# A two-layer hybrid encoder on one core: hi|lo side by side in the feed-forward, and the recurrence's cross-block products taken together

## Chip, core and metric

The kernel runs on one core of a Trainium2 chip. The metric is the device time of one execution in microseconds (us), median over the runs. In the profile TensorE is PE (its weight loads are PEld), VectorE is DVE, ScalarE is ACT, GpSimd is POOL, and SyncE, whose queue issues the weight DMAs, is SP. PSUM is the memory that TensorE writes its products to, in banks of 512 fp32 columns; the other operands lie in SBUF.

## What is computed

Two layers work on a residual stream x of 256 tokens by 1024 channels. Each layer projects x, runs three token mixers (pooling, windowed attention, and a gated linear recurrence in both directions), gates and merges them, and normalises. Then comes the feed-forward, 2816 wide:

```python
hidden = jax.nn.silu(x1 @ w_ffn_gate[i]) * (x1 @ w_ffn_up[i])
ffn = hidden @ w_ffn_down[i]
```

The recurrence, for 8 heads of 128 channels, with decays f = exp(log_f):

```python
b = jnp.cumsum(log_f)                 # within a chunk
att = (q * exp(b)) @ (k * exp(-b)).T  # kept where s <= t
o_intra = tril(att) @ v
o_inter = (q * exp(b)) @ state        # then: state = decay * state + kd.T @ v
```

It runs once forward and once over the flipped sequence, and both results are added. All operands are fp32.

## The kernel before

**Split operands.** A projection takes each fp32 operand as a hi and a lo part, both of type float32r, and computes hi x hi + hi x lo + lo x hi, three matmuls into one PSUM bank (`mm3`, lines 250 to 254). The activation's parts are the tiles `xh` and `xl`, [128, 8, 256] each: 8 blocks of 128 channels by 256 tokens.

**Weights.** All weights are listed as 214 chunks of 1 MB in the order of their use (lines 139 to 181). A chunk goes through three steps: `dma_chunk` issues its DMA on SP's queue into `raw`; `split_chunk` makes `whi` by a ScalarE copy (line 210) and `wlo` by a VectorE subtraction (line 211), and issues the DMA three chunks on; a product uses it (`use_chunk`). raw, whi and wlo have three buffers each, so the split of a chunk writes the buffer of the chunk that has just been used.

**Two forms of product.** `gemm_cols` (line 256) has weights stationary and 256 tokens moving: for two column blocks m and 8 channel blocks k, three matmuls of 256 columns into one half of a bank. `gemm_tok` (line 272) has activations stationary and 512 weight columns moving.

**The feed-forward** (lines 869 to 879): eleven pairs of products a layer, gate and up, each a `gemm_cols` into one bank of the pool `g`. ScalarE applies SiLU to the gate bank (line 873), VectorE multiplies it by the up bank (line 876), and `split_to` makes the hi part (ScalarE, line 293) and the lo part (VectorE, line 294) for the down projection.

**Background work.** Mixers are Python generators in the list `tasks`. After a projection `step_end` splits the next chunk and calls `background` (line 225): it draws on the first three tasks in turn until the costs that they yield reach a budget of 3000; `yield None` puts a task to sleep until the next step. This sets the order in which instructions are written; a list scheduler then orders each engine's instructions by readiness and by that priority.

**The recurrence** (`hgrn_task`, line 348) is one task for each two heads, four in a layer. The list `busy` lets one task at a time into its first part. For each direction d, VectorE forms decay products by two scans (Ct, Rt), two reciprocals into a tile `inv`, and from them QI, KI (inside a block of 64 tokens) and QL, KL (across blocks), tiles of a pool of seven buffers (`work`). After a sleep TensorE computes, all in plain fp32 (two matmul instructions a product): eight diagonal products of 64x64 (line 431), which alternate between the lower and the upper half of the output's partitions; four products of neighbouring blocks (line 439), the forward direction's all on the lower half, the backward direction's all on the upper one; and two products of 128x128 for blocks further apart (line 444). Then the task sleeps, and the other direction follows. At the end masks are applied, two products with v follow (lines 468, 469), a root mean square is formed with POOL's power (line 302, called at 478), the gate product is made (line 484), and the result is turned by TensorE (line 492).

## Time and profile before

| | |
|---|---|
| median of 3 runs | 1334.33 us (1334.32 to 1334.39) |
| the profiled execution | 1334.35 us |
| its span, first to last instruction | 1332.6 us |
| TensorE matmul, busy share | 98% |
| VectorE | 65% |
| ScalarE | 44% |
| POOL | 1% |
| mean granted TensorE clock | 0.996 of full speed |
| moved by DMA | 233 MB, 175 GB/s |

A share is that of the span. Matmuls are pipelined and their ends are modelled, so the distance between the starts of two is what they cost, and not the duration shown. The chain that ended last is followed back from the last instruction: at each step to whatever released it.

### The profile page before, as it was taken

What the parts mean: (1) busy time and instruction counts of PE and PEld (TensorE: products, weight loads), DVE (VectorE), ACT (ScalarE), POOL (GpSimd) and SP (SyncE); (2) the same over time, 40 slices, a digit from 0 to 9 for tenths busy, and PEclk for the clock granted to TensorE, in tenths of its full rate; (3) what the DMA queues carried; (4) which work ended last, traced back from release to release, by engine and by line L of the source; (5) the groups of instructions that cost most, each with busy time, mean ns of one, the idle gap of its engine ahead of it and who ended that gap; (6) DMA issues with size and microseconds to landing.
All of it is one profiled execution on the core that took longest, in us unless ns stands there. A gap on an engine that the chain in (4) does not pass through costs nothing.

```text
span 1332.6 us, 20047 instructions
## 1 busy us (share of the span) xinstructions
PE 1308.5 (98%) x8585; PEld 1185.8 (89%) x8585; DVE 867.5 (65%) x1126; ACT 587.1 (44%) x644; POOL 16.7 (1%) x24
## 2 busy tenths in 40 slices
PE   8999999999999999999989999999999999999997
PEld 6899999998888799998779999999988887999986
DVE  4598887575656855554555999875846658554445
ACT  5444444544444443443334444445534444444431
POOL 0000000000000000000000000000000000000000
PEclk9999999999999999999989999999999999999999
DMA  8654545244556475655356555442455664755551
GB/s 310 196 185 158 166 151 159 96 158 159 197 190 228 151 233 179 189 190 190 126 176 203 169 172 166 158 159 90 134 189 190 202 217 154 226 189 190 180 194 38
DMA packets 160280, 233.43 MB, mean 175 GB/s; under 512 B 3840, under 2 KB 108864, under 8 KB 160192
## 3 DMA queue, kind: packets, MB, share of 16 engines
q1 hardware_dynamic: 158496, 227.44, 51.6%
q10 hardware_dynamic: 1696, 4.72, 1.1%
q8 instruction: 67, 1.10, 0.3%
q14 instruction: 21, 0.17, 0.0%
HBM read 231.10 MB, written 1.05 MB: 174 GB/s over the span
## 4 chain that ended last, share of the span: by engine, by line
PE 93%; DVE 4%; ACT 1%; issue 1%; POOL 1%; DMA 0%; POOLq 0%; DVEq 0%; ACTq 0%
PE g L252 28%; PE g L253 28%; PE g L254 28%; DVE wlo L211 2%; PE t L444 1%; PE t L431 1%; PE t L439 1%; PE t L312 1%; POOL rs_y L302 1%; PE t L468 1%; PE t L469 1%; ACT whi L210 0%; DVE ln_st L326 0%; PE t L508 0%; PE t L528 0%
## 5 line engine op out<-in xcount | busy, mean ns | idle before, releaser
L211 DVE TENSOR_TENSOR wlo<-raw,whi 128x2048 fp32r<-128x2048 f32 (+2 forms) x218 | 489.8, 2249 | 347.4 <-ACT whi L210 347.0
L210 ACT ACTIVATE whi<-raw 128x2048 fp32r<-128x2048 f32 (+2 forms) x218 | 409.9, 1883 | 517.5 <-issue 220.7
L252 PE MATMUL g<-xh,whi 128*128 128x256 f32 x1600 | 455.6, 285 | 0.0
L254 PE MATMUL g<-xh,wlo 128*128 128x256 f32 x1600 | 453.1, 283 | 0.0
L253 PE MATMUL g<-xl,whi 128*128 128x256 f32 x1600 | 453.0, 283 | 0.0
L252 PEld LDWEIGHTS g<-xh,whi 128*128 128x128 f32 x1600 | 307.0, 192 | 0.2
L253 PEld LDWEIGHTS g<-xl,whi 128*128 128x128 f32 x1600 | 307.0, 192 | 0.2
L254 PEld LDWEIGHTS g<-xh,wlo 128*128 128x128 f32 x1600 | 306.9, 192 | 0.0
L252 PE MATMUL g<-whi,xh 128*128 128x512 f32 x480 | 190.2, 397 | 1.3 <-ACT whi L210 1.2
L253 PE MATMUL g<-wlo,xh 128*128 128x512 f32 x480 | 189.5, 395 | 1.4 <-DVE wlo L211 1.4
L254 PE MATMUL g<-whi,xl 128*128 128x512 f32 x480 | 188.1, 393 | 0.0
L253 PEld LDWEIGHTS g<-wlo,xh 128*128 128x128 f32 x480 | 91.8, 191 | 21.4 <-DVE wlo L211 3.1
L252 PEld LDWEIGHTS g<-whi,xh 128*128 128x128 f32 x480 | 91.8, 191 | 21.2 <-ACT whi L210 1.8
L254 PEld LDWEIGHTS g<-whi,xl 128*128 128x128 f32 x480 | 91.6, 191 | 19.1
L253 PE MATMUL g<-wlo,s 128*128 128x512 f32 x224 | 87.5, 391 | 0.0
L254 PE MATMUL g<-whi,s 128*128 128x512 f32 x224 | 87.5, 390 | 0.0
L252 PE MATMUL g<-whi,s 128*128 128x512 f32 x224 | 87.1, 390 | 0.0
L252 PE MATMUL g<-whi,sa 128*128 128x512 f32 x160 | 62.8, 393 | 0.0
L253 PE MATMUL g<-wlo,sa 128*128 128x512 f32 x160 | 62.5, 390 | 0.0
L254 PE MATMUL g<-whi,sb 128*128 128x512 f32 x160 | 62.3, 389 | 0.0
L253 PEld LDWEIGHTS g<-wlo,s 128*128 128x128 f32 x224 | 42.1, 188 | 9.0 <-DVE wlo L211 0.4
L254 PEld LDWEIGHTS g<-whi,s 128*128 128x128 f32 x224 | 42.0, 188 | 8.6
(168 smaller groups left out, 1136.2 us busy)
## 6 DMA issues: line engine op xcount, KB each, us to landing
raw<-in_w_in_dram SPq DMA_DIRECT2D x106, 1024.0 KB, 5.1
raw<-in_w_ffn_gate_dram SPq DMA_DIRECT2D x22, 1024.0 KB, 5.3
raw<-in_w_ffn_up_dram SPq DMA_DIRECT2D x22, 1024.0 KB, 5.3
raw<-in_w_ffn_down_dram SPq DMA_DIRECT2D x22, 1024.0 KB, 4.9
raw<-in_w_branch_c_dram SPq DMA_DIRECT2D x8, 1024.0 KB, 5.1
raw<-in_w_branch_a_dram SPq DMA_DIRECT2D x8, 1024.0 KB, 5.0
raw<-in_w_out_dram SPq DMA_DIRECT2D x8, 1024.0 KB, 4.9
raw<-in_w_ple_gate_dram SPq DMA_DIRECT2D x8, 1024.0 KB, 5.1
```

Source lines behind the costliest of these rows:

```text
L210: A.activation(out=hi[:, ks, :], in_=t[:, ks, :], func=AF.Copy)
L211: V.tensor_tensor(out=lo[:, ks, :], in0=t[:, ks, :], in1=f(hi[:, ks, :]), op=ALU.subtract)
L252: PE.matmul(ps, lhsT=ah, rhs=bh, start=first, stop=False)
L253: PE.matmul(ps, lhsT=ah, rhs=bl, start=False, stop=False)
L254: PE.matmul(ps, lhsT=al, rhs=bh, start=False, stop=last)
L302: G.tensor_tensor(out=y, in0=v, in1=mhalf.to_broadcast([P, n]) if n > 1 else mhalf, op=ALU.pow)
L312: PE.transpose(ps[:, k * P:(k + 1) * P], xt[:, t, (4 * hf + k) * P:(4 * hf + k + 1) * P], ident)
L431: PE.matmul(dg[po:po + 64, co:co + 64], lhsT=KI[:, cs], rhs=QI[:, cs], start=True, stop=True)
L439: PE.matmul(cr[po:po + 64, co:co + 64], lhsT=KL[:, h, 4 * t, :], rhs=QL[:, h, 4 * t, :], start=True, stop=True)
L444: PE.matmul(lg[:, co:co + P], lhsT=kp.rearrange("p b u -> p (b u)"), rhs=qp.rearrange("p b u -> p (b u)"), start=True, stop=True)
L468: PE.matmul(o, lhsT=at[:, 2 * h + t, :], rhs=vt[:, t, hs], start=True, stop=False)
L469: PE.matmul(o, lhsT=al[:, 2 * h + 1 - t, :], rhs=vt[:, 1 - t, hs], start=False, stop=True)
```

## The change

In the feed-forward the gate and up products use a new `gemm_wide`. `xh` and `xl` become two halves of one tile `xx`, [128, 8, 2, 256], so that for each k hi and lo of the activation stand side by side as 512 columns. The hi weights are multiplied by all 512 in one matmul, the lo weights by the 256 hi columns. Each m has a bank of its own; its first half holds hi x hi + lo x hi, its second hi x lo, and `joined` adds them: a ScalarE copy of the first half, then a VectorE addition of the second. The gate's banks come from the pool `g`, the up's from the pool `t`.

In the recurrence the first direction now computes only its diagonal products, and goes on to the second direction without the sleep. The second direction computes the neighbouring-block products of both directions, alternating between the lower and upper half of the output, and then all far ones. `inv` goes: the reciprocals are written into QI and KI and multiplied in place. `tot` becomes a small copy, and KL is allocated after QL has been formed. One sleep is added ahead of the gate product.

```diff
--- before.py
+++ after.py
@@ -260,6 +260,24 @@
                 mm3(ps[:, m * S:(m + 1) * S], (w[0][:, k, ms], w[1][:, k, ms]),
                     act(k), k == 0, k == nk - 1)
 
+    def gemm_wide(w, ps):
+
+
+        for m in range(2):
+            ms = slice(m * P, (m + 1) * P)
+            for k in range(KD):
+                wide = (ps[m], w[0][:, k, ms], xx[:, k].rearrange("p a t -> p (a t)"))
+                narrow = (ps[m][:, 0:S], w[1][:, k, ms], xx[:, k, 0, :])
+                for i, (o, a, b) in enumerate((wide, narrow) if k == 0 else (narrow, wide)):
+                    PE.matmul(o, lhsT=a, rhs=b, start=k == 0 and i == 0, stop=k == KD - 1 and i == 1,
+                              skip_group_check=True)
+
+    def joined(ps, dst):
+
+        for m in range(2):
+            A.activation(out=dst[:, m, :], in_=ps[m][:, 0:S], func=AF.Copy)
+            V.tensor_tensor(out=dst[:, m, :], in0=dst[:, m, :], in1=ps[m][:, S:2 * S], op=ALU.add)
+
     def xk(k):
         return xh[:, k, :], xl[:, k, :]
 
@@ -350,7 +368,7 @@
         while busy:
             yield None
         busy.append(hp)
-        dg = None
+        dg, across = None, []
         smask = kc[:, K_MASK:K_MASK + 512]
         emask = kc[:, K_MASK + 1:K_MASK + 513]
 
@@ -365,7 +383,7 @@
             e, la = (0, 1) if fwd else (1, 0)
             ft, kt = (ff, kf) if fwd else (fb, kb)
             f0 = ft[:, 1:513]
-            Ct, Rt, inv = work([P, 512]), work([P, 512]), work([P, 512])
+            Ct, Rt = work([P, 512]), work([P, 512])
             if fwd:
                 V.tensor_tensor_scan(out=Ct, data0=smask, data1=f0, initial=0.0, op0=ALU.max, op1=ALU.mult)
                 yield 600
@@ -378,29 +396,31 @@
                 V.tensor_tensor_scan(out=Rt, data0=ft[:, 0:512], data1=smask, initial=0.0,
                                      op0=ALU.mult, op1=ALU.max)
             yield 600
-            C, R, I, q3, k3 = c32(Ct), c32(Rt), c32(inv), c32(q), c32(kt)
-            V.reciprocal(out=I[:, :, e, :], in_=R[:, :, e, :])
+            QI, KI = work([P, 512]), work([P, 512])
+            C, R, q3, k3, q2, k2 = c32(Ct), c32(Rt), c32(q), c32(kt), c32(QI), c32(KI)
+            V.reciprocal(out=q2[:, :, e, :], in_=R[:, :, e, :])
             yield 1670
-            V.reciprocal(out=I[:, :, la, :], in_=C[:, :, la, :])
+            V.reciprocal(out=k2[:, :, la, :], in_=C[:, :, la, :])
             yield 1670
-            QI, KI = work([P, 512]), work([P, 512])
-            q2, k2 = c32(QI), c32(KI)
-            V.tensor_tensor(out=q2[:, :, e, :], in0=q3[:, :, e, :], in1=I[:, :, e, :], op=ALU.mult)
+            V.tensor_tensor(out=q2[:, :, e, :], in0=q3[:, :, e, :], in1=q2[:, :, e, :], op=ALU.mult)
             V.tensor_tensor(out=q2[:, :, la, :], in0=q3[:, :, la, :], in1=C[:, :, la, :], op=ALU.mult)
             yield 660
             V.tensor_tensor(out=k2[:, :, e, :], in0=k3[:, :, e, :], in1=R[:, :, e, :], op=ALU.mult)
-            V.tensor_tensor(out=k2[:, :, la, :], in0=k3[:, :, la, :], in1=I[:, :, la, :], op=ALU.mult)
+            V.tensor_tensor(out=k2[:, :, la, :], in0=k3[:, :, la, :], in1=k2[:, :, la, :], op=ALU.mult)
             yield 660
 
             u = 31 if fwd else 0
-            tot = c4(Ct)[:, :, :, :, u:u + 1]
+            tot = small([P, 2, 4, 2, 1], "tot")
+            V.tensor_copy(out=tot, in_=c4(Ct)[:, :, :, :, u:u + 1])
             QL = work([P, 2, 5, 64])
-            KL = work([P, 2, 5, 64])
+            KL = None
             qb = range(1, 4) if fwd else range(0, 3)
             kb_ = range(0, 3) if fwd else range(1, 4)
 
             for L, blks, src, intra, own, far, fac in (
                     (QL, qb, q, QI, e, la, Ct), (KL, kb_, kt, KI, la, e, Rt)):
+                if L is None:
+                    L = KL = work([P, 2, 5, 64])
                 for h in range(2):
                     b0 = blks[0]
                     cs = slice(h * S + 64 * b0, h * S + 64 * b0 + 192)
@@ -429,20 +449,24 @@
                     cs = slice(h * S + 64 * b, h * S + 64 * b + 64)
                     po, co = 64 * (b % 2), d * S + (2 * h + b // 2) * 64
                     PE.matmul(dg[po:po + 64, co:co + 64], lhsT=KI[:, cs], rhs=QI[:, cs], start=True, stop=True)
+            across.append((QL, KL))
             if d == 0:
-                cr, lg = tbank(), tbank()
+                continue
+            cr, lg = tbank(), tbank()
             for h in range(2):
                 for t in range(2):
 
-                    po = 0 if fwd else 64
                     co = (2 * h + t) * 64
-                    PE.matmul(cr[po:po + 64, co:co + 64], lhsT=KL[:, h, 4 * t, :], rhs=QL[:, h, 4 * t, :],
-                              start=True, stop=True)
-                qp = QL[:, h, 2:4, :] if fwd else QL[:, h, 1:3, :]
-                kp = KL[:, h, 1:3, :] if fwd else KL[:, h, 2:4, :]
-                co = (2 * h + d) * P
-                PE.matmul(lg[:, co:co + P], lhsT=kp.rearrange("p b u -> p (b u)"),
-                          rhs=qp.rearrange("p b u -> p (b u)"), start=True, stop=True)
+                    for po, (Q, K) in zip((0, 64), across):
+                        PE.matmul(cr[po:po + 64, co:co + 64], lhsT=K[:, h, 4 * t, :], rhs=Q[:, h, 4 * t, :],
+                                  start=True, stop=True)
+            for h in range(2):
+                for e, (Q, K) in enumerate(across):
+                    qp = Q[:, h, 2:4, :] if e == 0 else Q[:, h, 1:3, :]
+                    kp = K[:, h, 1:3, :] if e == 0 else K[:, h, 2:4, :]
+                    co = (2 * h + e) * P
+                    PE.matmul(lg[:, co:co + P], lhsT=kp.rearrange("p b u -> p (b u)"),
+                              rhs=qp.rearrange("p b u -> p (b u)"), start=True, stop=True)
             if d == 1:
                 busy.clear()
             yield None
@@ -477,6 +501,7 @@
         r = small([P, 4], "rms")
         rsqrt(r, ms, 4)
         yield 700
+        yield None
         for t in range(2):
             for h in range(2):
                 hs = slice((2 * hp + h) * P, (2 * hp + h + 1) * P)
@@ -583,7 +608,8 @@
         yield 600
 
 
-    xh, xl = slot("xh", [P, KD, S], F32R), slot("xl", [P, KD, S], F32R)
+    xx = slot("xx", [P, KD, 2, S], F32R)
+    xh, xl = xx[:, :, 0, :], xx[:, :, 1, :]
     load_x(0)
     dma_chunk()
     dma_chunk()
@@ -832,7 +858,8 @@
             for _ in held:
                 step_end()
 
-        xh, xl = slot("xh", [P, KD, S], F32R), slot("xl", [P, KD, S], F32R)
+        xx = slot("xx", [P, KD, 2, S], F32R)
+        xh, xl = xx[:, :, 0, :], xx[:, :, 1, :]
 
         def ln1(t, b):
             layer_norm(t, gb, [(xt[:, t, 512 * hf:512 * hf + 512], ALPHA, b[hf]) for hf in range(2)], transpose_x)
@@ -867,18 +894,21 @@
         hs = [slot(tag, [P, 2, 4, S], F32R) for tag in ("sa", "sb", "s4", "s5", "s8")]
         hs.append(slot("s7", [P, 2, 2, S], F32R))
         for c in range(NF // 2):
-            pg, pu = gbank(), gbank()
-            gemm_cols(use_chunk(), xk, pg)
-            s = misc([P, 2, S])
-            A.activation(out=s, in_=pg.rearrange("p (m t) -> p m t", t=S), func=AF.Silu)
+            pg, pu = [gbank(), gbank()], [tbank(), tbank()]
+            gemm_wide(use_chunk(), pg)
+            s, u = misc([P, 2, S]), misc([P, 2, S])
+            joined(pg, s)
+            A.activation(out=s, in_=s, func=AF.Silu)
             step_end()
-            gemm_cols(use_chunk(), xk, pu)
-            V.tensor_tensor(out=s, in0=s, in1=pu.rearrange("p (m t) -> p m t", t=S), op=ALU.mult)
+            gemm_wide(use_chunk(), pu)
+            joined(pu, u)
+            V.tensor_tensor(out=s, in0=s, in1=u, op=ALU.mult)
             i = 2 * (c % 2)
             split_to(hs[c // 2][:, 0, i:i + 2, :], hs[c // 2][:, 1, i:i + 2, :], s)
             step_end()
         gb = load_gb("s6", ln2_g[l], ln2_b[l])
-        xh, xl = slot("xh", [P, KD, S], F32R), slot("xl", [P, KD, S], F32R)
+        xx = slot("xx", [P, KD, 2, S], F32R)
+        xh, xl = xx[:, :, 0, :], xx[:, :, 1, :]
         last = l == DEPTH - 1
 
         def store(t, hf):
```

## Rows read from the trace of the kernel before

**Rows 1.** The page's chain that ended last, share of the span by engine.
```profile
PE 93%; DVE 4%; ACT 1%; issue 1%; POOL 1%; DMA 0%; POOLq 0%; DVEq 0%; ACTq 0%
```

**Rows 2.** Timeline of PE, two stretches: start us, us, engine, line, operation, tiles, shape.
```profile
399.69 0.39 PE L252 MATMUL g<-whi,xh 128*128 128x512 f32 x1
...
400.37 0.39 PE L252 MATMUL g<-whi,xh 128*128 128x512 f32 x1
...
486.03 0.28 PE L252 MATMUL g<-xh,whi 128*128 128x256 f32 x1
...
486.39 0.28 PE L252 MATMUL g<-xh,whi 128*128 128x256 f32 x1
```

**Rows 3.** Busy time by stretch, feed-forward: PE, PEld, DVE, ACT, POOL, then clock and DMA.
```profile
475.00:602.00 127.00, 127.00 (x1059) 126.95 (x1058) 66.48 (x45) 54.51 (x45) 0.00 (x0) 1.00 0.60 191
```

**Rows 4.** Timeline of PE, one direction's block in the recurrence.
```profile
88.60 0.28 PE L254 MATMUL g<-xh,wlo 128*128 128x256 f32 x1
88.81 0.69 PE L431 MATMUL t<-w 128*64 128x64 f32 x16
89.32 0.40 PE L439 MATMUL t<-w 128*64 128x64 f32 x4
89.65 0.49 PE L444 MATMUL t<-w 128*128 128x128 f32 x2
90.07 0.45 PE L439 MATMUL t<-w 128*64 128x64 f32 x4
90.44 0.49 PE L444 MATMUL t<-w 128*128 128x128 f32 x2
90.69 0.36 PE L252 MATMUL g<-xh,whi 128*128 128x256 f32 x1
90.89 0.28 PE L253 MATMUL g<-xl,whi 128*128 128x256 f32 x1
```

**Rows 5.** Timeline of PE, output products of the recurrence (L468, L469).
```profile
127.04 0.39 PE L468 MATMUL t<-s,m 128*128 128x128 f32 x2
127.27 0.39 PE L469 MATMUL t<-s,m 128*128 128x128 f32 x2
```

**Rows 6.** Groups by line: a 256-column ScalarE copy, a 256-column VectorE product.
```profile
L703 ACT ACTIVATE h<-g 128x256 f32<-128x256 f32 x48 | 15.5, 377 | 6.0 <-DVE w L411 6.0
...
L388 DVE TENSOR_TENSOR w<-h,w 128x256 f32<-128x256 f32 x16 | 6.7, 419 | 3.2 <-PE t L431 3.2
```

**Rows 7.** Timeline of ACT, then of DVE, in the feed-forward.
```profile
492.64 1.92 ACT L210 ACTIVATE whi<-raw 128x2048 fp32r<-128x2048 f32 x1 [3.33 <-PE g L253]
494.46 0.58 ACT L873 ACTIVATE m<-g 128x512 f32<-128x512 f32 x1
498.40 1.92 ACT L210 ACTIVATE whi<-raw 128x2048 fp32r<-128x2048 f32 x1 [3.36 <-issue]
500.22 0.61 ACT L293 ACTIVATE sa<-m 128x512 fp32r<-128x512 f32 x1
...
494.59 2.29 DVE L211 TENSOR_TENSOR wlo<-raw,whi 128x2048 fp32r<-128x2048 f32 x1 [2.87 <-ACT whi L210]
498.89 0.69 DVE L876 TENSOR_TENSOR m<-m,g 128x512 f32<-128x512 f32 x1 [2.01 <-PE g L254]
```

**Rows 8.** Line 439's matmuls: duration ns min/median/max, first and last start.
```profile
L439 PE MATMUL t<-w x128: 222/222/270, 89.3 to 906.4; 128*64 128x64 f32 x128
```

**Rows 9.** Busy time by stretch, the second layer's recurrence (columns as rows 3).
```profile
730.00:830.00 100.00, 100.00 (x745) 92.53 (x744) 94.33 (x165) 44.63 (x55) 1.01 (x1) 1.00 0.52 170
```

**Rows 10.** Waits: who waited for whom, us in total, times, longest.
```profile
DVE rs_t L304 <- POOL rs_y L302: 8.8, 15, 1.1
```

**Rows 11.** Timeline of PE at the boundary of the two layers.
```profile
674.42 1.97 PE L312 MATMUL t<-ident,x 128*128 128x128 f32 x8 [3.47 <-DVE x L337]
...
677.24 0.63 PE L252 MATMUL g<-whi,xh 128*128 128x512 f32 x1
677.66 0.63 PE L253 MATMUL g<-wlo,xh 128*128 128x512 f32 x1
```


## The prediction, made before the changed kernel was run

> **What bounds the kernel now.** I read the chain of waits first: TensorE's matmuls make up 93% of the chain that ended last, VectorE 4% [rows 1]. So a microsecond counts where TensorE's instructions come closer together, or where TensorE would wait for something new. Matmul durations in the timeline are modelled and overlap, so I read the distance between starts. Three 512-column products take 0.68 us of starts (399.69 to 400.37), and in the feed-forward three 256-column ones 0.36 us (486.03 to 486.39) [rows 2]. One of 512 columns (0.227) therefore costs less than two of 256 (0.24). The stage leaves much room beside TensorE: of 127 us VectorE works 66.5 and ScalarE 54.5 [rows 3]. The recurrence interrupts the projections with short blocks of small products, which I read as starts too [rows 4, 5].
>
> The sum is made against the profiled execution: 1334.35 us, with a span of 1332.6 us and 1.75 us around it. It stands 0.02 us above the median of the three runs, so no correction is needed.
>
> **Feed-forward, the products.** Before, each pair (m, k) has three 256-column products: 3 x 0.12 = 0.36 us. After, it has one of 512 columns and one of 256: 0.227 + 0.12 = 0.347 us. The columns streamed are the same, 768; one weight load and one instruction's fixed cost go, 0.013 us. There are 2 layers x 22 products x 16 pairs = 704 pairs: **-9.2 us**. Bounds: if the wide one took 0.24 us, as two narrow ones do, the gain is 0; if 0.226, 704 x 0.014 = 9.9 us. I take 0.013, since both shapes have their own rows, and only their taking turns has none. Putting hi and lo side by side in one tile moves no bytes and issues nothing.
>
> The row says 0.12 us for 256 columns and 0.227 for 512, hence a fixed part of 2 x 0.12 - 0.227 = 0.013 us for each instruction. The Trainium skill, TensorE: Matmul & The Clock Gate, section Back-to-back issue gap, speaks against this change: it gives a fixed part of 2.5 ns beside the columns. By that figure the feed-forward would save an estimated 1.8 us and the kernel would take 1323.9 us. The pitch in the rows is the measured one, and I go by it.
>
> **Feed-forward, the evacuation.** Each product now needs two ScalarE copies of 128x256 out of PSUM and two VectorE additions. A copy of that size takes 0.377 us and a VectorE two-input operation 0.419 us [rows 6]. Over one layer's 22 products: ScalarE 44 x 0.377 = 16.6 us more, 71 us of the 122 that the stage then lasts; VectorE 44 x 0.419 = 18.4 us more, 85 of 122. The sum costs them at nothing: both engines have the room, each half has a bank of its own, and banks come from two pools of four, so TensorE fills the next pair's while these are read. What could be late is the weights' splitting, queued behind on the same engines. Here the order counts: the split of the next weights (492.64, 498.40) is issued before the SiLU and before the hi part of the product, although the code writes those first [rows 7]. The issue order therefore follows readiness. The wlo of 494.59 ends at 496.88; its weights go into the buffer of the product that has just ended, and are needed two products later, at 492.6 + 2 x 5.76 = 504.1 us. That is 7.2 us of lead; ahead of it now come a copy and two additions, 1.2 us, and 0.4 us go as two products get shorter. About 5.6 us stay: 0 us on the path.
>
> **Recurrence, the products.** One direction's block before, from its rows [rows 4]: the last projection product starts at 88.60 and the next would at 88.72; the second one after the block starts at 90.89, so the first counts from 90.77. Block: 90.77 - 88.72 = 2.05 us, two per task 4.10. Inside: entering the 64-column mode 0.09; sixteen instructions of the diagonal products 0.51; four of neighbouring blocks and the change to 128 columns 0.33; two far ones and a change back 0.42; four neighbouring and a change 0.37; two far ones 0.25; 0.08 for the first projection's weights, which nothing hid. A modelled duration of a 64-column product is 0.222 us [rows 8], so first to last start is 0.69 - 0.22 = 0.47 for the sixteen diagonal ones (0.031 each: they alternate between both halves of the output) and 0.40 - 0.22 = 0.18 for the four neighbouring ones (0.059 each: all on one half).
> The change from 64 to 128 columns costs 0.33 - 0.18 = 0.15 to the next start, and 0.10 more behind it: the last two far ones and the projection's first weights take 0.25 + 0.08 = 0.33, where two products of that shape take 0.23 [rows 5].
> After, first direction: 0.09 + 0.47 + 0.15 + 0.10 = 0.81 us. Second direction: 0.09 + 0.51 + sixteen neighbouring ones, now alternating halves, at the diagonal's 0.47 + 0.25 for the change + eight far ones at half of 0.23, 0.89 = 2.21 us. Task: 3.02 against 4.10, saved 1.08. There are eight tasks, four in each layer (the 128 neighbouring instructions are sixteen for each [rows 8]): **-8.6 us**. Bounds: if the halves don't overlap, fifteen starts at 0.059 give 0.89 in place of 0.47, and the gain is 5.3 us; without the 0.10 behind the change, twice a task, it is 10.2.
>
> **Recurrence, the rest.** The inverse's tile goes; the reciprocals write into QI and KI: same operations. The copy of tot adds sixteen of VectorE's smallest operations, well below a 0.42 us one [rows 6], beside TensorE. QL and KL of the first direction now live into the second, so of seven buffers all are held; the second KI waits until the first diagonal products have read theirs, which are issued ahead of it. The sleep between the directions goes, so VectorE's work is offered a step earlier and stands denser. In the second layer VectorE is already busy 94.3 of 100 us [rows 9]. Four blocks there shorten by 2.2 us together, so it would stand at 95 of 97.8: still under TensorE. Cost 0, bound 4.3 us (the layer's own gain) if that room is not there.
>
> **The added sleep** puts the gate product one step later. Until then it stands in VectorE's queue behind POOL's power, for which VectorE waits 8.8 us in 15 times [rows 10]; whatever is queued behind it, wlo among it, is freed. It adds no instruction and no DMA. The transposes after it come one step later, for the last task too, but the removed sleep gave that step back. Cost 0; the bounds are one such wait for the last task, 8.8 / 15 = 0.6 us either way.
>
> **One thing moves with the clock of events.** At the layer boundary TensorE is idle 3.47 us, and its 512-column products then start 0.42 us apart, near twice 0.227: the lower of its two clock levels, 1.2 GHz [rows 11]. Nine of them follow in that view, 0.2 us too much each: 1.8 us. The boundary comes earlier now; the stretch may vanish or stretch: 0, within 2 us.
>
> **Sum:** 1334.35 - 9.2 - 8.6 = 1316.55; against the median, **1316.5 us**.
>
> **Rivals.**
> Forecast, both gains land: 0.70.
> *VectorE becomes the bound in the second layer's recurrence.* For it: the 94.3 of 100. Against: the room just worked out. The layer's 4.3 us are lost: 1320.8. Chance 0.13.
> *The merge saves nothing in the stream*, because the fixed part hangs on the columns: 1334.35 - 8.6 = 1325.7. Against it stand both pitches. Chance 0.07. The figure of TensorE: Matmul & The Clock Gate, section Back-to-back issue gap, in the Trainium skill falls close to this with its 1323.9.
> *The neighbouring products don't overlap* in spite of alternating: 1334.35 - 9.2 - 5.3 = 1319.8. Against: the diagonal ones do, with the same shapes. Chance 0.05.
> *Slower: the feed-forward hangs on a ring between ScalarE and VectorE.* If the copies, additions, SiLU and splits were issued in the order of the code, each waiting for the other engine, a gate product would need 2 x 0.38 + 2 x 0.42 + 0.58 + 1.92 + 2.29 = 6.39 us, and an up product 0.76 + 0.84 + 0.69 + 0.61 + 1.92 + 2.29 = 7.11: 13.5 us a pair. It decides from 11.1 us on, TensorE's own pair. Eleven pairs take 148.5 us against 126.7 now, less the 7.2 of lead: +14.6 a layer, +29.2, with the recurrence's gain 1354.9. Against: the order that the rows show [rows 7]. Chance 0.05.
>
> **How the numbers follow.** The low end takes every upper bound: 9.9 and 10.2, the 1.8 of the slow clock and the sleep's 0.6: 1311.8. The high end takes in the first three rivals: 1326. Outside lie the ring and the tails. About 0.2% (2.7 us) is what a measurement of this kernel can tell from no change. Faster by more holds all cases but the ring and a mixture of half a ring with half the gain: 0.92. Within 0.2%: 0.03. Slower: 0.05.
>
> **What would show it.** Right: in the feed-forward, starts alternating 0.12 and 0.227 us apart and 5.55 us a product; wlo still ending over 4 us before use; in the recurrence a block of 16 alone, and one of 16 diagonal, 16 neighbouring and 8 far instructions of about 2.2 us. Wrong: a pair at 0.36; neighbouring starts 0.058 apart throughout; TensorE waiting for wlo after 730 us or in the feed-forward; SiLU issued ahead of whi.

## The result, and the profile after

| | before | after |
|---|---|---|
| median in the comparison | 1334.36 us | 1319.25 us (1318.04 to 1319.50, 4 runs) |
| the profiled execution | 1334.35 us | 1319.02 us |
| its span | 1332.6 us | 1317.2 us |
| TensorE, VectorE, ScalarE busy | 98, 65, 44% | 98, 68, 47% |
| mean granted TensorE clock | 0.996 | 0.997 |

The ratio is 0.9885, with an interval of 0.9868 to 0.9902: faster by 15.1 us. The forecast was 1316.5 us with a range of 1311.8 to 1326.0, so direction and range held, and 2.5 to 2.7 us of the forecast gain are missing. TensorE is still the bound. The page's chain that ended last, which answers to [rows 1]:

```profile
PE 91%; DVE 6%; ACT 1%; issue 1%; POOL 1%; DMA 0%; POOLq 0%; SPq 0%; DVEq 0%; ACTq 0%
```

**Feed-forward.** PE's timeline of the changed kernel: the start of the first layer's 22 products, two pairs in the middle, and the start of the down projection behind them. Columns as in [rows 2], where the pair took 0.36 us.

```profile
472.17 0.39 PE L272 MATMUL g<-xx,whi 128*128 128x512 f32 x1
...
493.62 0.40 PE L272 MATMUL t<-xx,whi 128*128 128x512 f32 x1
493.85 0.28 PE L272 MATMUL t<-xx,wlo 128*128 128x256 f32 x1
493.97 0.39 PE L272 MATMUL t<-xx,whi 128*128 128x512 f32 x1
494.20 0.27 PE L272 MATMUL t<-xx,wlo 128*128 128x256 f32 x1
...
595.22 0.39 PE L252 MATMUL g<-whi,sa 128*128 128x512 f32 x1
```

The 22 products take 595.22 - 472.17 = 123.05 us, 5.593 each. Before they took 126.71 (475.24 to 601.95), 5.760 each. Over 44 products that is -7.3 us, where the forecast had -9.2. The mean over all starts of this line is 0.234 us for a wide matmul that a narrow one follows, and 0.116 for the narrow one: 0.350 a pair, not 0.347.

Busy time by stretch, the feed-forward and then the second layer's recurrence (columns as in [rows 3] and [rows 9]):

```profile
472.00:595.00 123.00, 123.00 (x706) 107.16 (x705) 82.64 (x88) 69.03 (x88) 0.00 (x0) 1.00 0.61 197
730.00:830.00 100.00, 99.75 (x787) 93.29 (x786) 94.54 (x177) 46.55 (x61) 3.58 (x2) 1.00 0.48 159
```

VectorE rose from 66.5 to 82.6 us and ScalarE from 54.5 to 69.0, while TensorE is busy for all of the 123. In the second line TensorE is no longer busy throughout: 0.25 us are missing.

The order on ACT and then on DVE in the feed-forward, which answers to [rows 7]:

```profile
494.74 0.39 ACT L278 ACTIVATE m<-t 128x256 f32<-128x256 f32 x1 [2.39 <-PE t L272]
495.02 1.91 ACT L210 ACTIVATE whi<-raw 128x2048 fp32r<-128x2048 f32 x1
496.83 0.61 ACT L311 ACTIVATE sa<-m 128x512 fp32r<-128x512 f32 x1
...
495.16 0.42 DVE L279 TENSOR_TENSOR m<-m,t 128x256 f32<-128x256 f32 x1 [1.17 <-ACT m L278]
495.62 0.69 DVE L905 TENSOR_TENSOR m<-m 128x512 f32<-128x512 f32 x1
496.97 2.29 DVE L211 TENSOR_TENSOR wlo<-raw,whi 128x2048 fp32r<-128x2048 f32 x1 [0.66 <-ACT whi L210]
```

The copy out of PSUM goes ahead of the next split, which goes ahead of the hi part, as forecast. wlo ends at 499.26; by the same count as in the prediction it is needed at 495.0 + 2 x 5.59 = 506.2. The lead is 6.9 us.

**Recurrence.** PE's timeline, the first direction's block and then the second's (answering to [rows 4]):

```profile
89.30 0.28 PE L254 MATMUL g<-xx,wlo 128*128 128x256 f32 x1
89.51 0.69 PE L451 MATMUL t<-w 128*64 128x64 f32 x16
90.12 0.39 PE L252 MATMUL g<-xx,whi 128*128 128x256 f32 x1
...
113.02 0.69 PE L451 MATMUL t<-w 128*64 128x64 f32 x16
113.53 0.64 PE L461 MATMUL t<-w 128*64 128x64 f32 x16
114.10 1.16 PE L468 MATMUL t<-w 128*128 128x128 f32 x8
115.01 0.36 PE L252 MATMUL g<-xx,whi 128*128 128x256 f32 x1
```

The sixteen neighbouring instructions (L461) now last 0.64 - 0.22 = 0.42 us from first to last start; in the single records the distances alternate between 6 or 7 and 51 or 52 ns. Worked out as in the prediction, the first block costs 0.81 and the second 2.17 us: 2.98 a task where it was 4.11 by the same reading of all blocks, so 1.13 x 8 = -9.0 us.

**Where the time went.** I compared how far TensorE is in the list of weight chunks in both traces. It is 0.70 us later than before by the end of the first value and gate projections (the first weights come in later); the recurrence and attention of the two layers take 3.83 and 3.74 us less, the feed-forwards 3.66 each, the boundary between the layers 1.13 less, and everything else is the same within 0.06. Sum: 0.70 - 7.57 - 7.32 - 1.13 = -15.32, and the last matmul starts at 1308.27 instead of 1323.58. The start and the boundary can't be put down to the change: the kernels of the next section, with the same code there, pass the start 0.1 to 1.2 us earlier than this one, and `no_added_sleep` and `wide_more` take 0.81 and 1.03 us more at the boundary. The blocks of the recurrence alone save 4.52 a layer, so 0.7 us a layer were given back there. The waits show to what in part (who waited for whom, us in total, times, longest):

```profile
PE t L553 <- DVE s L509: 1.3, 2, 0.7
PE t L492 <- DVE m L483: 0.4, 2, 0.2
...
DVE rs_t L322 <- POOL rs_y L320: 11.0, 16, 1.2
```

L553 is a transpose of the attention's scores, L509 the recurrence's gate product; the transposes wait up to 0.7 us in each layer. VectorE's timeline in the first layer, then PE's:

```profile
250.19 0.48 DVE L548 TENSOR_SCALAR m<-m,rd 128x512 f32<-128x512 f32 x1
250.59 1.12 DVE L509 SCALAR_TENSOR_TENSOR s<-t,rms,s 128x128 f32<-128x128 f32 x4
...
251.76 0.66 PE L553 MATMUL t<-ident,m 128*128 128x128 f32 x4 [0.60 <-DVE s L509]
```

The transposes' operand (L548) is ready at 250.67, but they start only when the gate product has ended, at 251.71. In the trace's records L548 updates no semaphore, and the next update of VectorE's is that of the last L509. Whether the transposes also need the PSUM bank that L509 reads, the trace does not tell. An idle time of PE is less than what it costs, so I read blocks by starts, as above: this one costs 1.25 us where four such transposes without a wait cost 0.44, and the block of output products at 122.5 (L492) costs 2.21 where others cost 1.79. Before, too, one block of transposes waited (0.5 a layer), which cost 0.64 in the first layer. The difference of these three, 0.82 + 0.43 - 0.64 = 0.6, is near the 0.7, though blocks are also cut differently in the two traces. VectorE's wait for POOL grew from 8.8 to 11.0 us [rows 10].

**Boundary.** PE's timeline between the layers, answering to [rows 11]:

```profile
667.76 1.75 PE L330 MATMUL t<-ident,x 128*128 128x128 f32 x8 [3.54 <-DVE x L355]
...
670.16 0.63 PE L252 MATMUL g<-whi,xx 128*128 128x512 f32 x1
670.59 0.63 PE L253 MATMUL g<-wlo,xx 128*128 128x512 f32 x1
...
671.44 0.48 PE L252 MATMUL g<-whi,xx 128*128 128x512 f32 x1
```

The wait of 3.5 us is the same. The starts 0.43 us apart that follow it, the lower level of 1.2 GHz, end at 671.44, 3.7 us after the transposes begin. In the trace of before they end at 680.23, 5.8 us after. But `no_added_sleep`, whose code at the boundary is the same as the changed kernel's, runs at the lower level until 672.86, 4.9 us after its transposes begin, and `ffn_only` and `rec_only` both gain 1.2 us here. So the 1.1 us can't be put down to either part of the change.

### The profile page after: what moved, and what is told of

Read it like the earlier page. It is cut to its first block, busy times and chain, and to the rows that moved or that the text cites. A ratio compares the mean times of both kernels' runs of the same rounds, so it can differ in the third digit from the quotient of the medians.

```text
span 1317.2 us, 18830 instructions
## 1 busy us (share of the span) xinstructions
PE 1292.2 (98%) x7881; PEld 1140.0 (87%) x7881; DVE 900.2 (68%) x1230; ACT 617.4 (47%) x732; POOL 20.0 (2%) x24
## 4 chain that ended last, share of the span: by engine, by line
PE 91%; DVE 6%; ACT 1%; issue 1%; POOL 1%; DMA 0%; POOLq 0%; SPq 0%; DVEq 0%; ACTq 0%
PE g L252 22%; PE g L253 22%; PE g L254 22%; PE t L272 9%; PE g L272 9%; DVE wlo L211 2%; ACT whi L210 1%; PE t L451 1%; POOL rs_y L320 1%; PE t L492 1%; PE t L493 1%; PE t L468 0%; PE t L330 0%; DVE ln_st L344 0%; PE t L533 0%
## 5 line engine op out<-in xcount | busy, mean ns | idle before, releaser
L252 PE MATMUL g<-xx,whi 128*128 128x256 f32 x896 | 256.9, 287 | 0.0
L253 PE MATMUL g<-xx,whi 128*128 128x256 f32 x896 | 253.9, 283 | 0.0
L254 PE MATMUL g<-xx,wlo 128*128 128x256 f32 x896 | 253.7, 283 | 0.0
L252 PE MATMUL g<-whi,xx 128*128 128x512 f32 x480 | 189.5, 395 | 1.7 <-ACT whi L210 1.6
L253 PE MATMUL g<-wlo,xx 128*128 128x512 f32 x480 | 189.2, 394 | 1.4 <-DVE wlo L211 1.4
L254 PE MATMUL g<-whi,xx 128*128 128x512 f32 x480 | 188.0, 393 | 0.0
L252 PEld LDWEIGHTS g<-xx,whi 128*128 128x128 f32 x896 | 171.7, 192 | 0.7
L253 PEld LDWEIGHTS g<-xx,whi 128*128 128x128 f32 x896 | 171.8, 192 | 0.2
L254 PEld LDWEIGHTS g<-xx,wlo 128*128 128x128 f32 x896 | 171.6, 192 | 0.0
L272 PE MATMUL t<-xx,whi 128*128 128x512 f32 x352 | 123.6, 396 | 0.0
L272 PE MATMUL g<-xx,whi 128*128 128x512 f32 x352 | 123.6, 396 | 0.0
L252 PEld LDWEIGHTS g<-whi,xx 128*128 128x128 f32 x480 | 91.6, 191 | 21.5 <-ACT whi L210 2.2
L253 PEld LDWEIGHTS g<-wlo,xx 128*128 128x128 f32 x480 | 91.6, 191 | 21.0 <-DVE wlo L211 2.6
L254 PEld LDWEIGHTS g<-whi,xx 128*128 128x128 f32 x480 | 91.3, 190 | 18.9
L272 PE MATMUL g<-xx,wlo 128*128 128x256 f32 x352 | 90.9, 279 | 0.0
L272 PEld LDWEIGHTS g<-xx,whi 128*128 128x128 f32 x352 | 64.5, 188 | 12.0
```

The source lines that it names most:

```text
L252: PE.matmul(ps, lhsT=ah, rhs=bh, start=first, stop=False)
L253: PE.matmul(ps, lhsT=ah, rhs=bl, start=False, stop=False)
L254: PE.matmul(ps, lhsT=al, rhs=bh, start=False, stop=last)
L272: PE.matmul(o, lhsT=a, rhs=b, start=k == 0 and i == 0, stop=k == KD - 1 and i == 1, skip_group_check=True)
```

## The experiments

Every time is a median of four or five runs, and its ratio is to the kernel before on the same chip (medians 1333.13 to 1333.77 us there). Traces are compared by chunk progress, as above, since the start differs by up to 1.2 us between executions.

### Each part alone

`ffn_only` is the kernel before with the feed-forward's part of the diff; `rec_only` is the changed kernel with the feed-forward of before.

```diff
 ffn_only (against before)
-            gemm_cols(use_chunk(), xk, pg)
+            gemm_wide(use_chunk(), pg)
...
 rec_only (against after)
-            gemm_wide(use_chunk(), pg)
+            gemm_cols(use_chunk(), xk, pg)
```

> The kernel before with the feed-forward part alone (xx, wide products, joined), the recurrence as before. Theory (the two parts add up, nothing is shared): the feed-forward's products start 5.593 us apart as in the changed kernel, 44 x 0.167 = 7.3 us less than before: 1327.0 us. Rival (the parts share VectorE, and one hides or spoils the other's gain): further than 1.5 us from that.

> The kernel before with the recurrence's part alone (order of the small products, inverse's tile, sleeps), the feed-forward as before. Theory: eight tasks save 1.13 us of blocks each, 9.0 us, and 0.7 us a layer goes to new waits of TensorE there, so 1334.4 - 7.7 = 1326.7 us, and both single gains add up to the 15 us of the change. Rival (the 0.7 us a layer come from the other part, through tiles and buffers): 1325.3 us.

Measured: `ffn_only` 1326.37 us, ratio 0.9945 (0.9933 to 0.9958), 7.4 us less; `rec_only` 1325.76 us, 0.9939 (0.9927 to 0.9952), 8.0 us less. The parts add up to 15.4, near the whole change's 15.1. By the traces each part alone is also 1.2 us shorter at the boundary, which is not its own, so that the two sums agree to 0.3 us is partly chance. In `ffn_only` each feed-forward is 3.66 us shorter, and no recurrence stretch moves by more than 0.02 us. In `rec_only` the stretches of the recurrence and attention are within 0.02 us of those of the changed kernel, and the same wait stands in its list, with its own line numbers:

```profile
PE t L535 <- DVE s L491: 1.3, 2, 0.7
```

So the 0.7 us a layer were lost inside the recurrence's part, and don't come from the two parts meeting.

### The neighbouring products, one half after the other

```diff
-            for h in range(2):
-                for t in range(2):
-                    for po, (Q, K) in zip((0, 64), across):
+            for po, (Q, K) in zip((0, 64), across):
+                for h in range(2):
+                    for t in range(2):
```

> The changed kernel, but the sixteen neighbouring-block instructions of a task run first all on the lower half of the output, then all on the upper. Theory (alternating halves lets two run side by side): starts 0.058 us apart in place of 7 and 52 ns in turn, so sixteen take 0.87 in place of 0.45 us, 8 x 0.4 = 3.3 us slower than the changed kernel: 1322.5 us. Rival (the gain is only that of fewer changes between 64 and 128 columns): no slower than 1319.5 us.

Measured: 1320.58 us, 0.9901 (0.9888 to 0.9915). PE's timeline of the second block:

```profile
113.19 0.92 PE L461 MATMUL t<-w 128*64 128x64 f32 x16
114.04 1.16 PE L468 MATMUL t<-w 128*128 128x128 f32 x8
```

First to last start is 0.92 - 0.22 = 0.70 us against 0.42 alternating: 0.28 x 8 = 2.25 us of blocks; the span grew by 1.5 us against the changed kernel once the start is taken out. Two of the eight blocks cost nothing, one in each layer, since the wait behind them gets shorter by as much (the output products of the first layer's take 1.93 us where they took 2.21). The result lies between the two expectations: taking turns is what saves, but giving it up doesn't lose all of it. Without any overlap fifteen starts at 0.058 would need 0.88. The single records explain the rest: four distances of 58 or 59 ns, then seven of 4 to 6 or 52 to 55, then four of 58 or 59 again. That fits an upper half that starts beside the fifth product instruction of the lower one; the records don't name the half, so this is read from the distances.

### Wide and narrow in groups

```diff
-            for k in range(KD):
-                for i, (o, a, b) in enumerate((wide, narrow) if k == 0 else (narrow, wide)):
+            for i in range(2):
+                for k in range(KD):
+                    o, a, b = (wide, narrow)[i]
```

> The changed kernel, but for each m the eight wide products of the feed-forward run first, then the eight narrow ones. Theory A (taking turns is what costs the missing 2.6 ns a pair): wide ones 0.227, narrow ones 0.120 us apart, a product 5.55 us, 1.9 us faster than the changed kernel, 1317.4 us. Theory B (a wide one costs 0.233 with these operands whatever stands beside it): 0.233 within the group, a product 5.59 us or more, no faster than 1319 us.

Measured: 1318.22 us, 0.9885 (0.9869 to 0.9900), not told apart from the changed kernel by the ratio. By the trace a product takes 5.585 us, so the feed-forward gains 0.17 us a layer more. PE's timeline:

```profile
495.77 1.12 PE L273 MATMUL g<-xx,wlo 128*128 128x256 f32 x8
496.72 2.00 PE L273 MATMUL g<-xx,whi 128*128 128x512 f32 x8
498.56 1.12 PE L273 MATMUL g<-xx,wlo 128*128 128x256 f32 x8
```

Eight wide ones take 498.56 - 496.72 = 1.84 us, 0.230 each, eight narrow ones 0.95, 0.119 each. Inside a group, on the mean of all groups, the first wide ones take 0.234, 0.236, 0.228, 0.232 and 0.231, the last three 0.226 to 0.227. The price of the row of before is reached only some five instructions behind a change from narrow to wide. Neither theory as I had put it: grouping pays, but a fifth of what was missing. Groups of sixteen, in `best_pool` below, gain 0.61 us a layer, two thirds of it.

### Without the join

```diff
-            joined(pg, s)
-            A.activation(out=s, in_=s, func=AF.Silu)
+            for m in range(2):
+                A.activation(out=s[:, m, :], in_=pg[m][:, 0:S], func=AF.Silu)
```

> The changed kernel, but the second half of the feed-forward's banks is not added: SiLU and the gate product read the first half out of PSUM, so the term hi x lo of gate and up is left out of the result. Theory (copies and additions are hidden beside TensorE): products 5.593 us apart as with them, no faster than 0.5 us. Rival (the evacuation holds TensorE's next products, or their weights, and takes back a part of the gain): products nearer 5.55 us apart, up to 1.9 us faster.

Measured: 1318.47 us, 0.9888 (0.9874 to 0.9901). The starts of all wide and narrow matmuls sum to 245.63 us in both traces, so the copies and additions cost nothing there. The profiled execution is 1.27 us faster than the changed kernel's, and 1.1 of that lie in the start, which comes earlier in this trace.

### The two sleeps

Three kernels: the added sleep out; the removed sleep back beside it; and both as before.

```diff
 no_added_sleep, sleeps_as_before
-        yield None
         for t in range(2):
...
 sleep_back, sleeps_as_before
             if d == 0:
+                yield None
                 continue
```

> The changed kernel without the added sleep ahead of the gate product. Theory (the sleep is worth nothing on TensorE's path, as forecast: 0, within 0.6 us): within 1 us of the changed kernel, 1318 to 1320 us. Rival A (it keeps TensorE's transposes of the gate product from waiting for VectorE): over 1 us slower. Rival B (it is what puts the new waits into the recurrence, 0.7 us a layer): 1.4 us faster, 1317.8 us.

> The changed kernel with the sleep between the two directions put back. Theory (the missing sleep makes VectorE's work denser, and so the output products wait for it: 0.35 us by the trace at 122 and 776 us, and the rest of 0.7 us a layer): the waits shrink, up to 1.4 us faster, 1317.8 us. Rival (the waits hang on where a task's later steps fall, not on this sleep): within 0.5 us of the changed kernel or slower.

> The changed kernel with both sleeps as they were before: the one between the directions put back, the added one taken out. Without the added one alone the changed kernel was 6.2 us of span slower. Theory A (the added sleep is needed because the missing one makes VectorE's work denser): with both as before the transposes wait little, within 1.5 us of the kernel with both sleeps (1317.4 us). Theory B (the added sleep is worth its 6 us by itself, whatever the other does): 1323 us or more.

| | median, us | ratio |
|---|---|---|
| no_added_sleep | 1325.38 | 0.9939 (0.9927 to 0.9952) |
| sleep_back | 1317.36 | 0.9881 (0.9866 to 0.9897) |
| sleeps_as_before | 1318.26 | 0.9888 (0.9873 to 0.9903) |

Taken out alone, the added sleep costs 6.1 us by the medians. By the traces the recurrence and attention of the two layers take 1.3 and 5.2 us more and the boundary 0.8, and the start is 1.1 us earlier. The trace of `no_added_sleep`, first a line of its waits:

```profile
PE t L516 <- DVE s L508: 5.2, 5, 2.0
```

Then VectorE's timeline in the second layer, and PE's beside it:

```profile
827.78 0.10 DVE L324 TENSOR_SCALAR rs_t<-rs_t 128x4 f32<-128x4 f32 x1
827.80 1.74 DVE L403 RECIPROCAL w<-w 128x256 f32<-128x256 f32 x1
...
830.64 2.29 DVE L211 TENSOR_TENSOR wlo<-raw,whi 128x2048 fp32r<-128x2048 f32 x1
832.84 0.16 DVE L325 TENSOR_TENSOR rms<-rs_t,rs_y 128x4 f32<-128x4 f32 x1
...
833.25 1.12 DVE L508 SCALAR_TENSOR_TENSOR s<-t,rms,s 128x128 f32<-128x128 f32 x4
...
833.65 0.48 PE L516 MATMUL t<-ident,s 128*128 128x128 f32 x1 [1.96 <-DVE s L508]
...
835.85 0.41 PE L253 MATMUL g<-xx,whi 128*128 128x256 f32 x1
836.06 0.41 PE L254 MATMUL g<-xx,wlo 128*128 128x256 f32 x1
```

The busy time by stretch there (the last three columns are the granted clock, the DMA share and GB/s):

```profile
832.00:838.00 6.00, 4.35 (x24) 4.35 (x25) 6.00 (x15) 1.70 (x4) 0.00 (x0) 0.72 0.52 175
```

The same for the stretch behind another of these waits, of 1.35 us, in the first layer:

```profile
137.20:143.20 6.00, 5.99 (x28) 5.05 (x29) 5.70 (x18) 1.52 (x4) 0.00 (x0) 1.00 0.72 245
```

TensorE's transposes wait for the gate product, which waits for the root mean square's last step (L325), which stands behind 5 us of other work on VectorE: the step before it (L324) ends at 827.88, it starts at 832.84, and a split of weights of 2.29 us is the longest piece between. VectorE is busy all the while. Behind this wait of 1.96 us the 256-column starts lie 0.21 us apart instead of 0.12, and the granted clock of the stretch is 0.72: TensorE went on at its lower level until 836.9. This late product costs twice. The one with the wait of 1.35 us does not: behind it the granted clock stays at 1.00.

With the other sleep put back and the added one still out (`sleeps_as_before`) the same gate product is not waited for so long, and the time is 1318.26 us:

```profile
PE t L517 <- DVE s L509: 1.0, 2, 0.5
```

So the added sleep is needed because the other one was removed. With both (`sleep_back`) the recurrence stretches are 0.35 and 0.41 us shorter than in the changed kernel: about half of the 0.7 us that were given back. Neither the wait of L553 nor that of the output products is in its list. The medians of these two and of the changed kernel are not told apart by their intervals; the steps in the trace are.

### The wide form elsewhere

`wide_more` uses `gemm_wide` for the attention's q and k and for the pooling, sixteen more products a layer. `best_all` adds the sleep and puts all sixteen wide matmuls ahead of the sixteen narrow ones; `best_late` is the same without the wide form in the first half of the attention; `best_pool` without it in the attention at all.

```diff
 best_pool: after, with sleep_back's line and
-        for m in range(2):
-            ms = slice(m * P, (m + 1) * P)
-            for k in range(KD):
+        for i in range(2):
+            for m in range(2):
+                ms = slice(m * P, (m + 1) * P)
+                for k in range(KD):
...
-            gemm_cols(use_chunk(), xk, ps)
+            gemm_wide(use_chunk(), ps)
-            A.activation(out=a[:, :, 8:264], in_=ps.rearrange("p (m t) -> p m t", t=S), func=AF.Copy)
+            joined(ps, a[:, :, 8:264])
```

> The changed kernel with the wide products also for the attention's q and k and for the pooling, 16 products a layer, joined on ScalarE and VectorE. Theory (each saves the feed-forward's 0.167 us where VectorE has room, 26 of 41 us at the end of this stretch): 32 x 0.167 = 5.3 us faster, 1314 us. Rival (VectorE, with 16 x 0.84 us more a layer in a stretch where it is busy 80 to 90%, falls behind, and TensorE waits): gains under 2 us or slower than the changed kernel.

> The changed kernel with the sleep between the directions put back, the wide products also for q, k and pooling, and in every wide product all sixteen wide matmuls ahead of the sixteen narrow ones. Theory (each saves on its own: 0.4 us a layer by the sleep, 2.4 us a layer by the 16 wide products as in the first layer of the run before, whose second layer lost 3.8 us to one wait for VectorE, and 0.02 us a product where the width changes twice and not four times): 1334 - 15.3 - 0.8 - 4.8 - 1.5 = 1312 us. Rival (the wait of the second layer returns): 1315 us or more.

> As the one before, but with the wide products for the second pair of heads and the pooling alone, 10 products a layer, where VectorE is less busy. Theory (VectorE's room decides): the second layer has no wait over 1 us, 20 x 0.15 = 3 us saved over the sleep's 0.8 and the grouping's 1.4: 1313.5 us. Rival (waits fall by chance, wherever steps end): a wait of over 1 us somewhere in the recurrence's or the attention's stretch, 1315 us or more.

> The changed kernel with the sleep between the directions put back, all sixteen wide matmuls of a product ahead of its sixteen narrow ones, and, beyond the feed-forward, the wide form for the pooling product alone; attention as in the changed kernel. Theory: what spoiled the two runs before this one was the narrow and wide order or the wide form in the attention, whose copies and additions stand in the queues that the recurrence's operations wait in; without it the gains add: 1317.4 with the sleep back, less 0.6 a layer from the grouped products, less 1.0 a layer from the pooling: 1314.2 us (1313.0 to 1315.5), with no TensorE wait over 0.9 us between 200 and 240 us. Rival: the waits of those runs do not come from the attention but from the pooling product and the sleep standing together, and come back: 1317 us or more, with a wait of over 1 us for VectorE between 200 and 240 or between 860 and 895 us.

| | median, us | ratio |
|---|---|---|
| wide_more | 1316.61 | 0.9874 (0.9861 to 0.9888) |
| best_all | 1322.06 | 0.9916 (0.9902 to 0.9929) |
| best_late | 1323.05 | 0.9919 (0.9906 to 0.9931) |
| best_pool | 1315.43 | 0.9868 (0.9851 to 0.9884) |

`wide_more` gained 2.4 us in the first layer's attention and pooling, against the changed kernel, and lost 2.5 in the second layer's attention before its pooling gained 1.3; the boundary took 1.0 more. Its trace there, VectorE's timeline and then PE's:

```profile
836.48 1.22 DVE L388 TENSOR_TENSOR_SCAN w<-kc,h 128x512 f32<-128x512 f32 x1
837.62 2.26 DVE L211 TENSOR_TENSOR wlo<-raw,whi 128x2048 fp32r<-128x2048 f32 x1
839.80 0.48 DVE L441 TENSOR_TENSOR w<-w,t 128x128 f32<-128x128 f32 x2
...
840.34 1.41 PE L468 MATMUL t<-w 128*128 128x128 f32 x6 [1.59 <-DVE w L441]
```

The busy time of the stretch behind it:

```profile
838.00:844.00 6.00, 4.41 (x28) 3.86 (x25) 5.96 (x11) 3.19 (x5) 0.00 (x0) 0.72 0.49 158
```

The far products' operand (L441) stands behind a scan and a split; TensorE waits 1.59 us and goes on at the lower level, with a granted clock of 0.72 over the stretch. It is the same pattern as in `no_added_sleep`, on another operand.

Against `sleep_back`, `best_all` and `best_late` lose 3.8 and 4.5 us in the first layer's attention and about as much in the second, to several waits and to the slower clock behind them. From the waits of `best_late` between 205 and 240 us:

```profile
PE t L452 <- DVE w L410: 0.9, 1, 0.9
PE g L273 <- DVE h L741: 0.6, 2, 0.4
PE t L470 <- ACT m L557: 0.4, 1, 0.4
PE t L463 <- DVE w L434: 0.4, 1, 0.4
```

And the busy time of the stretch that follows most of them:

```profile
234.00:240.00 6.00, 5.05 (x35) 3.99 (x35) 5.95 (x24) 1.77 (x5) 0.00 (x0) 0.72 0.56 179
```

L741 is the addition that the wide form brings to the attention; L410 and L434 form operands of the recurrence, on the same engine. None of the waits is over 0.9 us, but three of them (L470, L452, L463) fall between 232.7 and 235.6 us, and the granted clock of the stretch is 0.72, as behind the two longer ones. `best_pool` has none of these waits, as its theory had it (the time is at the upper end of that theory's range), and against `sleep_back` it gains 0.76 us a layer in the pooling and 0.61 in the feed-forward, and nothing in the attention. Its interval overlaps that of the changed kernel; its span, 1312.9 us against 1317.2, is the shortest of all. By the median it is the fastest version, and the steps say where from.

## Why the prediction was right, and where it was not

**Feed-forward, the products: right in kind, a term mis-sized.** The step that failed is "I take 0.013, since both shapes have their own rows, and only their taking turns has none". Taking turns has a price: the wide one takes 0.234 and not 0.227, the narrow one 0.116 and not 0.12. The pair saves 0.010, the kernel 7.3 us and not 9.2. `ffn_only` shows it by itself, and with groups of sixteen (`best_pool`) two thirds of the missing 1.9 us come back. The bound of 0 (a wide one at 0.24) and the value taken did hold it between them. Why the first wide ones behind a narrow one are dearer is open; `grouped` only shows where it falls.

**The rivals on the merge.** The merge saves 7.3 us, which rules out the rival of 1325.7. The Trainium skill, TensorE: Matmul & The Clock Gate, section Back-to-back issue gap, gives a fixed part of 2.5 ns for an isolated matmul, by which an estimated 1.8 us would have been saved; the rows show four times that, and the measurement decides.

**Feed-forward, the evacuation: right.** The order came as forecast, the lead is 6.9 us where 5.6 were expected, and `no_join` shows the cost of 0. The ring that would have made the kernel slower did not form: the split goes ahead of the hi part of the product, as [rows 7] had it.

**Recurrence, the products: right.** Forecast -8.6, measured -9.0: the neighbouring sixteen took 0.42 and not 0.47. `halves_apart` shows that without alternating a task's blocks save 0.85 us and not 1.13. These 0.85 come with the new order, which has fewer changes between shapes, and with the overlap that is left around the change of half; no run takes the two apart. The bound without overlap (5.3) was too far, since two halves in sequence overlap in part.

**"Recurrence, the rest": wrong by 0.7 us a layer.** The step put it at 0, because VectorE's 95 of 97.8 us would still be under TensorE. That room is an average. VectorE still has 5 us in 100 free, and yet single products come late, since each operand that TensorE needs stands behind whatever VectorE was given before it. `sleep_back` shows that about half is the price of the missing sleep between the directions. The other half was not pursued; its cause stays open.

**The added sleep: 0 as a pair, 6 alone.** "The removed sleep gave that step back" is what the three kernels show. But the bounds of 0.6 us either way were far too narrow: they took POOL's wait for the price, while the price was 5 us of VectorE's work in front, a weight split among it, and the slower clock behind.

**What moves with the clock of events: within its 2 us, by chance.** The boundary gave 1.1 us, the later start took 0.7. Other runs with the same code there show either value of the boundary and earlier starts, so that these two partly cancel is luck. Without them the kernel gains 14.9 us, and 2.9 of the forecast are missing.

The sum of the differences against the forecast of 17.8 us: 1.9 (products), -0.4 (blocks), 1.5 (waits), -1.1 (boundary), 0.7 (start): 2.6 of rounded terms, and 2.5 were missing between the two traces.

## What to carry to other kernels

Price a merged instruction from rows in the order in which it will run: the pitch of a stream of one shape is a bound, and not the value, for two shapes that take turns. Where the second engine is busy over 90%, read for each operand that the first engine awaits what stands ahead of it in the queue; the share of busy time says nothing of that, and one sleep, without an instruction more or less, was worth six microseconds. Extend a form that pays only where the engine that has to evacuate it has room: the same wide product gained in the pooling and the feed-forward. In the attention, beside the recurrence, it gained 1.0 us in one layer and lost in all the other trials.

## What the runs showed of the hardware that was not expected

- Small products on one half of the output and then on the other seem to overlap by themselves around the change, as read from the distances (`halves_apart`: seven distances of 4 to 6 or 52 to 55 ns among those of 58).
- A 512-column matmul behind 256-column ones takes 0.234 us and comes down to 0.227 over some five instructions (`grouped`), at full granted clock.
- Some waits in the middle of dense work were followed by TensorE's lower clock level. Behind waits of 1.96 us (`no_added_sleep`) and 1.59 us (`wide_more`), and with three of 0.4 to 0.9 us close together (`best_late`), stretches of 6 us had a mean granted clock of 0.72; the first lost about as much again as the wait itself. Behind a wait of 1.35 us in `no_added_sleep` the clock stayed at 1.00.
